# A decoder trunk in float32 parts: 18 of 22 gate and up tiles of each feed-forward block by Strassen's algorithm over halves, and the second product in four sections

## The chip, the cores and the metric

One core of a Trainium2 chip runs the whole program in one launch. The metric is device time in microseconds (us), the median of several runs; the profile is one further execution with the hardware profiler on. TensorE (PE) multiplies, VectorE (DVE), ScalarE (ACT) and GpSimd (POOL) do the elementwise work, and SyncE (SP) issues the large transfers.

## The reference, cut to what matters

Two layers, each a feed-forward block, a mixer and a second feed-forward block: four feed-forward blocks in all. The change touches these; the mixer keeps its arithmetic.

```python
D_MODEL, SEQ, DEPTH, D_FF, FFN_HALF = 1024, 512, 2, 2816, 0.5

def swiglu(h, w_in, w_out):
    gate, up = jnp.split(h @ w_in, 2, axis=-1)
    return (jax.nn.silu(gate) * up) @ w_out

for l in range(DEPTH):
    x = x + FFN_HALF * swiglu(rmsnorm(x, ffn1_norm[l]), ffn1_w_in[l], ffn1_w_out[l])
    x = x + hybrid_mixer(rmsnorm(x, mix_norm[l]), ...)
    x = x + FFN_HALF * swiglu(rmsnorm(x, ffn2_norm[l]), ffn2_w_in[l], ffn2_w_out[l])
```

## The kernel before

Activations lie feature-major: 8 tiles of [128 features, 512 tokens]. Every float32 operand is split into a high and a low part (`wh`, `wl` of a weight, `xh`, `xl` of the stream, `hh`, `hl` of the hidden layer), and a product is three matmuls, high by high, high by low and low by high (`mm3`).

A feed-forward block (`ffn`) has 22 feature tiles of the hidden layer. For each, `proj` makes the gate and then the up tile: 8 row tiles by 3 matmuls of 512 columns each, the weight stationary and the stream moving. The product's bank `pf` is then worked off: `t = pf * r` and `t = pf * t` on DVE, the SiLU on ACT, `t * r` on POOL, and the split into `hh` (ACT) and `hl` (DVE). The second product follows once all 22 are there: 8 output tiles, each a chain of 22 by 3 matmuls of 512 columns in one bank, added to the stream by one DVE instruction.

Weights come through SP, 512 KB at a time, into `raw` (2 slots). `convert` makes `wh` on ACT and `wl = raw - wh` on DVE (3 slots each); so each chunk of [128, 1024] numbers costs one ACT and one DVE instruction beside the 24 matmuls that use it. `convert` runs ahead of the product by these slots.

`Weave` sets the order in which instructions are written out on each engine, with a rough price list: chains of small steps (`weave.spawn`, `yield`) are placed between the matmuls, and `idle` lets work that is not urgent wait for its engine. Each engine then works in that order and waits by semaphores. The mixer uses the same `proj` and also `proj_tm`, whose matmuls have 256 moving columns with the stream stationary.

All instructions go through one recording helper, so that nearly all rows of the profile name its line (L246 here): tiles tell them apart.

Of the kernel before, what the change touches and what calls it, by code (L numbers as in the profile page):

```python
# [40 lines left out]

class Weave:
    """Emission order: chains of small dependent steps between the dense products.

    A chain is a generator that emits a step and yields the time in ns that
    has to pass before its next step beyond what its instructions take. A
    model of the engines, with rough prices of the instructions, tells when
    a chain's last step is through; the dense products, which call tick, fill
    the time in between."""

    COST = {"tensor": (1, 0.417), "vector": (70, 1.04), "scalar": (100, 0.84), "gpsimd": (120, 1.3)}
    HOP = 250.0         # from an engine to what another one does with its result
# [46 lines left out]
    def charge(self, engine, op, outs, ins, func=None):  # L99
# [20 lines left out]
        else:  # L120
# [3 lines left out]
            # columns of scalars, and sums  # L124
# [46 lines left out]
    def both(self, *chains):  # L171
        """One chain out of several."""
# [12 lines left out]
    def after(self, ticket, chain):  # L185
        """The chain, once the last one with this ticket is done."""
# [13 lines left out]
    def then(self, ticket, chain):  # L200
        """The chain, once the last one with this ticket so far is done."""
# [9 lines left out]
    def idle(self, engine, limit=800):  # L211
        """Wait, in a chain, for the engine to run dry, but not for long."""
# [10 lines left out]
class Engine:  # L223
    """An engine whose instructions the model takes down."""
# [26 lines left out]
class Pool:  # L251
    """A tile pool whose tiles the model takes down."""
# [12 lines left out]
    def room(self, tag, bufs=None):  # L265
        """Wait, in a chain, for the next slot of a ring."""
# [18 lines left out]

class Trunk:
    def __init__(self, ctx, tc, depth, w):
        self.tc = tc
        self.nc = self.weave = Weave(tc.nc)
        self.w = w  # L290
# [17 lines left out]
        self.chunks = self.weight_order(depth)  # L308
        self.raws = []
        self.parts = []  # L310
        self.converted = self.used = 0
        self.r = None
        self.evacs = [0, 0]     # of products: called for, emitted
# [8 lines left out]
    def select(self, name, compare, base, cm, step, out=None):  # L322
        """A mask: 1 where base + cm * partition + step * column compares so with 0."""
# [11 lines left out]
    def columns(self, name, ap):  # L335
        """Per-feature vectors, turned so that features lie on partitions."""
# [22 lines left out]
    def more_constants(self, vecs, a_log, dt_bias):  # L359
# [15 lines left out]
        # rows of the identity by quarter: [32 q + blk, a, i] = (i == 8 q + a)  # L375
# [7 lines left out]
        # a_log and dt_bias on every partition  # L383
# [25 lines left out]
    def load_x(self, x, gain):  # L409
        """The stream, feature-major, and with it the first two units of the first product."""  # L410
# [3 lines left out]
        with self.pool("xin", 1) as xin:  # L414
# [9 lines left out]
            for k in range(KD + 4):  # L424
# [11 lines left out]
                # the second unit two tiles behind the first  # L436
# [5 lines left out]
            self.used += 2  # L442
# [47 lines left out]
    def finish_norm(self):  # L490
        """r = (mean of squares + eps) ** -0.5 on every partition; one Newton step."""
# [20 lines left out]
    def weight_order(self, depth):  # L512
        """(matrix, first row tile, row tiles, first column, columns) in the order of use."""
        w = self.w

        def ffn(w_in, w_out):
            for f in range(KF):
                yield w_in, 0, KD, f * P, P
                yield w_in, 0, KD, DFF + f * P, P
            for n in range(KD):  # L520
                for k0, nk in OUT_SPLIT:
                    yield w_out, k0, nk, n * P, P
# [34 lines left out]
    def ahead(self):  # L557
        """Have the oldest chunk that has been fetched split into hi and lo parts."""
        self.weave.spawn(self.weave.after("hi", self.convert()))

    def split_chunk(self, engine):
        """The same at once, the low part by the engine given."""
        nc = self.nc
        raw = self.raws.pop(0)
        self.converted += 1
# [5 lines left out]
        return wh, wl  # L571

    def convert(self):
        nc = self.nc
        if not self.raws:
            return
        # a slot is free once the products with what it held have been emitted
        while self.converted - self.used >= 3:
            yield 300
        self.converted += 1  # L580
        raw = self.raws.pop(0)
        nk, n = raw.shape[1], raw.shape[2]
        if n == 16:
            # few columns: the parts side by side, for two passes over x instead of three
            both = self.wp.tile([P, nk, 2 * n], F32R, tag="wh", bufs=3, name="wb")
            wh, wl = both[:, :, 0:n], both[:, :, n:2 * n]
        else:
            wh = self.wp.tile([P, nk, n], F32R, tag="wh", bufs=3, name="wh")
            wl = self.wp.tile([P, nk, n], F32R, tag="wl", bufs=3, name="wl")
# [3 lines left out]
        def lo():  # L593
            yield from self.weave.idle("vector", LO_WAIT)
            nc.vector.tensor_tensor(wl, raw, wh.bitcast(F32), op=ALU.subtract)
            self.parts.append((wh, wl) if n > 16 else (both, None))
            self.fetch()
# [22 lines left out]
    def bank(self, shape, n=1):  # L620
        """A bank for a product, when n are free."""
# [3 lines left out]
    def evac(self, engine, f):  # L625
        """f, which reads the bank of a product, when the engine has time."""
# [8 lines left out]
    def proj(self, xs=None, units=1):  # L635
        """The next chunks of P columns, feature-major; the last row tile of all comes last."""
        xh, xl = xs or (self.xh, self.xl)
        ws, pss = [], []
        for u in range(units):
            wh, wl = self.next_weights()  # L640
            ps = self.bank([P, SEQ])
            last = KD if units == 1 else KD - 1
            for k in range(last):
                if k == 2:
                    self.ahead()
                self.used += k == KD - 1
                self.weave.until(lambda: len(xl) > k and xl[k] is not None)
                self.mm3(ps, (wh[:, k, :], wl if wl is None else wl[:, k, :]), (xh[k], xl[k]), k == 0, k == KD - 1)
            ws.append((wh, wl))
            pss.append(ps)  # L650
        if units > 1:
            k = KD - 1
            self.weave.until(lambda: len(xl) > k and xl[k] is not None)
            for (wh, wl), ps in zip(ws, pss):
                self.mm3(ps, (wh[:, k, :], wl if wl is None else wl[:, k, :]), (xh[k], xl[k]), False, True)
            self.used += units
        return pss if units > 1 else pss[0]

    def proj_tm(self, ready=lambda: True):
        """256 columns, token-major: two PSUM tiles [P, 2, 256], tokens (2 a + b) P + p."""  # L660
        nc = self.nc
        out = [self.bank([P, 2, 256], 2) for _ in range(2)]
        for k0 in (0, 4):
            wh, wl = self.next_weights()
# [15 lines left out]
            self.used += 1  # L680
# [4 lines left out]
    def ffn(self, hid, finish, first=None):  # L685
        nc = self.nc
        hh, hl = [], []
        first = first or self.proj(units=2)
        self.need_r()
        r = self.r  # L690

        def hidden(f, t):
            h = hid.tile([P, SEQ], F32R, name=f"hh{f}")
            l = hid.tile([P, SEQ], F32R, name=f"hl{f}")
# [815 lines left out]
```

## Time and profile before

| | |
|---|---|
| runs timed | 3, median 2834.55 us (2833.79 to 2834.58) |
| span of the profiled execution | 2834.2 us |
| busy share of the span | PE 99%, weight loads 83%, DVE 56%, ACT 45%, POOL 11% |
| granted TensorE clock | 0.998 of 2.4 GHz over the whole span |
| moved by transfers | 312 MB, mean 110 GB/s |
| stretch of a feed-forward block | about 360 us, four times |
| stretch of a mixer | about 680 us, twice |

The page gives no time for the profiled execution but its span, from its first to its last instruction; that is 0.35 us under the median of the timed runs, so span and time are taken as one number below. Busy shares are means over stages; PE's busy time includes the overlap of matmuls that follow each other, whose ends are modelled. The pace of matmuls is therefore read from the distance of their starts.

### The profile page before, as it was taken

The numbers are of one execution on the slowest core, as the hardware profiler recorded it, in microseconds if no ns is written. First come the engines' busy times: TensorE is split into PE (matmuls) and PEld (weight loads), VectorE is DVE, ScalarE is ACT, GpSimd is POOL, SyncE is SP. The second block draws the span as 40 slices with busy tenths as digits, with TensorE's granted clock in tenths as the row PEclk, the third lists the DMA queues.
The fourth block names the chain that finished last, engine by engine and source line by source line (L and its number), as shares of the span: only waits on it lengthen the run. The fifth ranks groups of instructions, "written<-read, shape, count | busy, mean of one in ns | idle before, by whom it ended". The sixth has DMA issues, their size and how long they took to land.

```text
span 2834.2 us, 38189 instructions
## 1 busy us (share of the span) xinstructions
PE 2803.1 (99%) x14638; PEld 2366.0 (83%) x14638; DVE 1578.3 (56%) x2646; ACT 1267.8 (45%) x2663; POOL 315.4 (11%) x312
## 2 busy tenths in 40 slices
PE   8999999999999999999999999999999999999999
PEld 6888888888888888888888888889988888888887
DVE  5444356987777544443344433678878765544422
ACT  4322236767664543222232222368675745422221
POOL 2110010000100031110011100110001002311100
PEclk9999999999999999999999999999999999999999
DMA  4333333323335743333333333323323349333332
GB/s 128 90 98 102 114 96 88 94 79 88 91 96 178 241 153 93 97 97 97 98 96 97 97 106 107 105 81 84 102 79 99 106 149 302 92 104 97 97 106 80
DMA packets 511223, 312.09 MB, mean 110 GB/s; under 512 B 31050, under 2 KB 481344, under 8 KB 511040
## 3 DMA queue, kind: packets, MB, share of 16 engines
q1 hardware_dynamic: 510704, 309.51, 37.1%
q8 instruction: 116, 1.90, 0.3%
q14 instruction: 67, 0.55, 0.1%
q10 hardware_dynamic: 336, 0.13, 0.0%
HBM read 276.03 MB, written 33.55 MB: 109 GB/s over the span
## 4 chain that ended last, share of the span: by engine, by line
PE 90%; DVE 6%; ACT 3%; issue 1%; DMA 0%; POOL 0%; SPq 0%; DVEq 0%; ACTq 0%; POOLq 0%
PE pf L246 82%; PE sbo_ps L246 1%; ACT u L246 1%; DVE sbs L246 1%; PE pq L246 1%; DVE itmp L246 1%; DVE wl L246 1%; DVE qkv L246 1%; PE z_ps L246 1%; PE pa L246 1%; DVE it L246 1%; PE at_ps L246 1%; PE pp L246 0%; PE py L246 0%; PE qk_ps L246 0%
## 5 line engine op out<-in xcount | busy, mean ns | idle before, releaser
L246 DVE TENSOR_TENSOR wl<-raw,wh 128x1024 fp32r<-128x1024 f32 (+1 forms) x463 | 596.4, 1288 | 484.8 <-ACT wh L246 483.1
L246 PE MATMUL pf<-xh,wh 128*128 128x512 f32 x2176 | 854.4, 393 | 0.2 <-DVE t L246 0.2
L246 PE MATMUL pf<-xh,wl 128*128 128x512 f32 x2176 | 852.4, 392 | 1.6 <-DVE wl L246 1.6
L246 PE MATMUL pf<-xl,wh 128*128 128x512 f32 x2176 | 853.4, 392 | 0.0
L246 ACT ACTIVATE wh<-raw 128x1024 fp32r<-128x1024 f32 (+1 forms) x464 | 481.1, 1038 | 294.2 <-PE pf L246 228.1
L246 PEld LDWEIGHTS pf<-xh,wl 128*128 128x128 f32 x2176 | 409.0, 188 | 88.1 <-DVE wl L246 3.9
L246 PEld LDWEIGHTS pf<-xh,wh 128*128 128x128 f32 x2176 | 409.2, 188 | 83.5 <-issue 1.1
L246 PEld LDWEIGHTS pf<-xl,wh 128*128 128x128 f32 x2176 | 409.2, 188 | 83.2 <-issue 1.4
L246 PE MATMUL pf<-hl,wh 128*128 128x512 f32 x704 | 274.5, 390 | 0.0
L246 PE MATMUL pf<-hh,wh 128*128 128x512 f32 x704 | 273.9, 389 | 0.0
L246 PE MATMUL pf<-hh,wl 128*128 128x512 f32 x704 | 273.9, 389 | 0.0
L246 PE MATMUL pf<-wh,xh 128*128 128x256 f32 x768 | 226.3, 295 | 0.0
L246 PE MATMUL pf<-wl,xh 128*128 128x256 f32 x768 | 218.2, 284 | 0.0
L246 PE MATMUL pf<-wh,xl 128*128 128x256 f32 x768 | 218.0, 284 | 0.0
L246 POOL TENSOR_TENSOR t<-t,r 128x512 f32<-128x512 f32 x88 | 114.1, 1296 | 816.4 <-ACT t L246 816.4
L246 ACT ACTIVATE t<-t 128x512 f32<-128x512 f32 x88 | 55.6, 632 | 330.8 <-DVE t L246 330.8
L246 ACT ACTIVATE hh<-t 128x512 fp32r<-128x512 f32 x88 | 55.6, 632 | 321.9 <-DVE t L246 321.9
L246 PEld LDWEIGHTS pf<-hh,wl 128*128 128x128 f32 x704 | 132.2, 188 | 27.4
L246 PEld LDWEIGHTS pf<-hh,wh 128*128 128x128 f32 x704 | 132.2, 188 | 27.3
L246 PEld LDWEIGHTS pf<-hl,wh 128*128 128x128 f32 x704 | 132.2, 188 | 27.2
L246 PEld LDWEIGHTS pf<-wh,xl 128*128 128x128 f32 x768 | 148.0, 193 | 1.7
L246 PEld LDWEIGHTS pf<-wh,xh 128*128 128x128 f32 x768 | 147.9, 193 | 1.8
(1049 smaller groups left out, 3621.0 us busy)
## 6 DMA issues: line engine op xcount, KB each, us to landing
raw<-in_ffn_w_in_dram SPq DMA_DIRECT2D x176, 512.0 KB, 3.9
raw<-in_w_in_dram SPq DMA_DIRECT2D x144, 512.0 KB, 3.9
raw<-in_ffn_w_out_dram SPq DMA_DIRECT2D x64, 512.0 KB, 4.1
raw<-in_ffn_w_out_dram SPq DMA_DIRECT2D x32, 384.0 KB, 3.4
gsp<-gt SPq DMA_DIRECT2D x32, 256.0 KB, 3.3
of<-osp SPq DMA_DIRECT2D x32, 256.0 KB, 4.3
raw<-in_w_branch_b_dram SPq DMA_DIRECT2D x16, 512.0 KB, 4.2
raw<-in_w_branch_a_dram SPq DMA_DIRECT2D x16, 512.0 KB, 5.2
```

The source lines that it names most:

```text
L246: return f(*args, **kw)
```

## The change

Of the 22 gate and up tile pairs of a block, 4 stay as they were. The other 18 are done two at a time in 9 groups. For a group, the weights are taken as 2 by 2 blocks (gate and up by the two halves of the 1024 inputs, each [4 row tiles, 256 columns]) and the stream as 2 by 2 blocks (halves of the inputs by halves of the 512 tokens). The Winograd form of Strassen's algorithm makes the product from 7 block products in place of 8. Each is 2 feature tiles by 4 row tiles by 3 matmuls of 256 columns: 168 matmuls of 256 columns for a group, in place of 96 of 512.

For this the four weight blocks of a group (`sraw`, 8 slots) get four sums on POOL (`sums`, `last_sum`), and each of the 7 operands is split by `convert` into `wh` and `wl`. The stream is normalized at the start (`xs`, on DVE), its four sums are made on POOL, and the high and low parts of the sums (`halves`) and of the normalized stream (`replace`) are made once a block. Products gather in the banks `pq`, `ps` and `pf`; partial results are copied out by ACT (`m1`, `u2`, `u3`) or added by DVE (`t`, `up1`).

The second product comes in four sections of 4, 6, 6 and 6 hidden tiles, the first before the groups, the others between and after them, each added to the stream by DVE. `PLAN` sets this order. Weights of the second product and of the groups use a fourth pair of slots. In the mixer the one step that reads the beta and decay columns goes through the queue of evacuations.

```diff
-OUT_SPLIT = ((0, 8), (8, 8), (16, 6))
+H = SEQ // 2
+FC = 4
+NQ = (KF - FC) // 2
+SECTIONS = ((0, 4), (4, 6), (10, 6), (16, 6))
+RAWQ = 8
+HOME = {1: 11, 2: 12, 3: 12, 4: 22, 5: 0, 6: 11, 7: 21}
...
+    plan = [("c", u) for u in range(2 * FC)]
+    plan += down(0, (0, 1), 2) + down(0, range(2, KD))
+    plan += [("s", 0, 1), ("s", 0, 5)]
+    for q in range(NQ - 1):
+        plan += [("s", q, 2), ("s", q, 6), ("s", q + 1, 1), ("s", q, 7), ("s", q + 1, 5), ("s", q, 4), ("s", q, 3)]
+        if q in (3, 6):
+            plan += down(q // 3, range(KD))
...
+    def sums(self, q):
...
+        nc.gpsimd.tensor_tensor(t[0], t[21], t[22], op=ALU.add)
...
+        nc.gpsimd.tensor_tensor(t[21], t[11], t[21], op=ALU.subtract)
...
+        while 1 not in f.events:
+            yield 300
+        nc.gpsimd.tensor_tensor(t[11], t[0], t[11], op=ALU.subtract)
...
+    def last_sum(self, q):
...
+        self.nc.gpsimd.tensor_tensor(t[12], t[12], t[11], op=ALU.subtract)
...
+    def halves(self, hid):
...
+            nc.vector.scalar_tensor_tensor(xs[k // 4][:, k % 4, :], self.x[k], self.gain(k), self.r,
+                                           op0=ALU.mult, op1=ALU.mult)
...
+        for i, a, b in ((7, b22, b12), (5, b12, b11), (6, b22, b12), (4, b21, raw[6])):
+            yield 0
+            nc.gpsimd.tensor_tensor(raw[i], a, b, op=ALU.subtract)
...
+    def replace(self):
...
+            nc.scalar.activation(xh, src, AF.Copy)
+            yield 0
+            nc.vector.tensor_tensor(xl, src, xh.bitcast(F32), op=ALU.subtract)
...
+    def of_four(self, ps, i, start):
...
+                for n, (w, x) in enumerate(((wh, xh), (wh, xl), (wl, xh))):
+                    nc.tensor.matmul(ps[:, f, :], w[:, k, cols], x, start=start and f + k + n == 0,
+                                     stop=k == 3 and n == 2, skip_group_check=True)
...
+            if i == 1:
+                s["Q"] = self.sps.tile([P, 2, H], F32, tag="sp", name="pq")
+                self.of_four(s["Q"], 1, True)
+                s["m1"] = small("m1")
+                nc.scalar.copy(s["m1"], s["Q"])
...
+            elif i == 6:
+                self.of_four(s["Q"], 6, False)
+                s["u2"] = small("u2")
+                nc.scalar.copy(s["u2"], s["Q"])
...
+                    nc.scalar.copy(u3, s["Q"])
+                    s["up1"] = small("up1")
+                    nc.vector.tensor_tensor(s["up1"], s["S"], u3, op=ALU.add)
...
+            elif i == 4:
+                self.of_four(s["Q"], 4, False)
+                t = s["g0"]
+                nc.vector.tensor_tensor(t, s["Q"], t, op=ALU.mult)
```

On DVE, in the steady part of the gate and up tiles of the first block: before, the rows of one hidden tile (two chunks of weights, two steps on the bank `pf`, one low part `hl`).

```order
L246 TENSOR_TENSOR wl<-raw,wh 128x1024
L246 TENSOR_TENSOR t<-pf,r 128x512
L246 TENSOR_TENSOR wl<-raw,wh 128x1024
L246 TENSOR_TENSOR t<-pf,t 128x512
L246 TENSOR_TENSOR hl_899<-t,hh_898 128x512
```

In the change, the rows of one whole group at the same place (`sraw` and `s` are weight blocks and their sums, `hp` the hidden layer's parts, `u`, `m` and `up` partial results).

```order
L279 TENSOR_TENSOR t<-pf,m_1010 128x512
L279 TENSOR_TENSOR wl<-sraw,wh 128x1024
L279 TENSOR_TENSOR hp<-t,hp 128x2x256
L279 TENSOR_TENSOR wl<-s_1066,wh 128x1024
L279 TENSOR_TENSOR wl<-sraw,wh 128x1024 x2
L279 TENSOR_TENSOR up_1277<-ps,u_1275 128x512
L279 TENSOR_TENSOR wl<-sraw,wh 128x1024 x2
L279 TENSOR_TENSOR t<-pq,t 128x512
L279 TENSOR_TENSOR hp<-t,hp 128x2x256
L279 TENSOR_TENSOR t<-ps,u_1209 128x512
L279 TENSOR_TENSOR wl<-sraw,wh 128x1024
L279 TENSOR_TENSOR t<-t,up_1277 128x512
```

Two hidden tiles took 10 DVE rows before, 4 of them low parts of weights; a group for two hidden tiles takes 14, 7 of them low parts of weights, and the steps on the banks stand between these in one order.

On POOL, in the first block: before, the last constants, then the gate's `t * r` of 16 hidden tiles, then the sums of squares that follow the block.

```order
L246 MEMSET i_732 128x256
L246 AFFINE_SELECT i_732<-i_732 32x256 x4
L246 TENSOR_TENSOR t<-t,r 128x512 x16
L246 TENSOR_TENSOR ssq<-ssq,sq 128x512 x7
L246 MEMSET zero 128x128
```

In the change, at the same place, the sums of the weight blocks of two groups and a half.

```order
L279 AFFINE_SELECT i_792<-i_792 32x256 x4
L279 TENSOR_TENSOR s_819<-sraw 128x1024
L279 TENSOR_TENSOR sraw<-sraw 128x1024 x2
L279 TENSOR_TENSOR sraw<-s_819,sraw 128x1024
L279 TENSOR_TENSOR s_1066<-sraw 128x1024
L279 TENSOR_TENSOR sraw<-sraw 128x1024 x2
L279 TENSOR_TENSOR sraw<-s_1066,sraw 128x1024
```

Where one instruction on 512 columns stood for a hidden tile, four on 1024 columns stand for a group of two.

On ACT, in the change, between the product 5 of one group and the copy `u3` of the next (`wh` are the high parts of weights, here of a sum and of blocks):

```order
L279 ACTIVATE wh<-s_1066 128x1024
L279 COPY u_1209<-pq 128x512
L279 ACTIVATE wh<-sraw 128x1024
L279 COPY m_1243<-pq 128x512
L279 ACTIVATE wh<-sraw 128x1024
L279 COPY u_1275<-pq 128x512
```

The copies out of the bank `pq`, before which TensorE may not go on in that bank, stand behind high parts of weights that are themselves waiting for sums and slots; before, no copy of this kind stood in a block.

## Rows read from the trace of the kernel before

**Rows 1.** The page: busy time, share of the span and instructions by engine.
```profile
PE 2803.1 (99%) x14638; PEld 2366.0 (83%) x14638; DVE 1578.3 (56%) x2646; ACT 1267.8 (45%) x2663; POOL 315.4 (11%) x312
```

**Rows 2.** Engines by stretch (feed-forward blocks and mixers): us, busy us, clock, DMA share, GB/s.
```profile
35.00:386.00 351.00, 350.99 (x1542) 287.26 (x1543) 144.40 (x158) 104.86 (x132) 43.16 (x43) 1.00 0.35 101
386.00:1066.00 680.00, 671.96 (x4104) 582.74 (x4103) 490.15 (x1004) 417.22 (x1061) 76.82 (x85) 1.00 0.41 121
...
1427.00:1787.00 360.00, 360.00 (x1587) 296.56 (x1586) 148.70 (x156) 105.74 (x133) 37.77 (x32) 1.00 0.35 101
```

**Rows 3.** The chain that ended last: start, us, what, number of matmuls.
```profile
635.99 7.20 PE pf L246 x60
...
1427.79 359.12 PE pf L246 x1584
```

**Rows 4.** Groups by line on TensorE: shape, count, busy us, mean ns, idle before.
```profile
L246 PE MATMUL pf<-xh,wh 128*128 128x512 f32 x2176 | 854.4, 393 | 0.2 <-DVE t L246 0.2
...
L246 PE MATMUL pf<-wh,xh 128*128 128x256 f32 x768 | 226.3, 295 | 0.0
```

**Rows 5.** Groups by line and form on DVE, ACT and POOL, 1428 to 1787 us.
```profile
L246 DVE TENSOR_TENSOR wl<-raw,wh 128x1024 fp32r<-128x1024 f32 x59 | 77.5, 1313 | 93.6 <-ACT wh L246 93.6
L246 DVE TENSOR_TENSOR hl<-t,hh 128x512 fp32r<-128x512 f32 x22 | 15.2, 692 | 14.7 <-ACT hh L246 14.7
L246 DVE TENSOR_TENSOR t<-pf,t 128x512 f32<-128x512 f32 x22 | 15.2, 692 | 37.4 <-PE pf L246 35.3 <-POOL t L246 2.1
...
L246 DVE SCALAR_TENSOR_TENSOR xl<-x,v_nm,xh 128x512 fp32r<-128x512 f32 x8 | 6.0, 752 | 6.3 <-ACT xh L246 6.3
L246 DVE SCALAR_TENSOR_TENSOR x<-pf,x 128x512 f32<-128x512 f32 x8 | 5.5, 691 | 15.2 <-PE pf L246 15.2
...
L246 ACT ACTIVATE wh<-raw 128x1024 fp32r<-128x1024 f32 x59 | 61.8, 1049 | 55.3 <-PE pf L246 54.5 <-DMA raw<-in_ffn_w_in_dram 0.8
L246 ACT ACTIVATE hh<-t 128x512 fp32r<-128x512 f32 x22 | 13.9, 632 | 82.1 <-DVE t L246 82.1
...
L246 POOL TENSOR_TENSOR t<-t,r 128x512 f32<-128x512 f32 x22 | 28.5, 1293 | 205.7 <-ACT t L246 205.7
```

**Rows 6.** Groups by line over the span: a POOL instruction of 1024 columns; an ACT copy from a bank.
```profile
L246 POOL TENSOR_TENSOR wl<-raw,wh 128x1024 fp32r<-128x1024 f32 x1 | 2.4, 2388 | 11.2 <-ACT wh L246 11.2
...
L246 ACT COPY sraw<-pf 128x512 f32<-128x512 f32 x32 | 20.2, 630 | 0.0
```

**Rows 7.** Timeline of DVE and POOL where both work: start us, us, instruction.
```profile
13.32 0.75 DVE L246 SCALAR_TENSOR_TENSOR xl<-xps,v_n,xh 128x512 fp32r<-128x512 f32 x1 [1.41 <-ACT xh L246]
...
13.99 0.68 DVE L246 COPY x<-xps 128x512 f32<-128x512 f32 x1
...
980.79 1.29 POOL L246 TENSOR_TENSOR ga<-ga,yb 128x512 f32<-128x512 f32 x1 [1.32 <-DVE ga L246]
980.80 2.36 DVE L246 TENSOR_TENSOR wl<-raw,wh 128x1024 fp32r<-128x1024 f32 x1 [0.15 <-ACT wh L246]
...
1001.23 1.30 POOL L246 TENSOR_TENSOR yb<-yb,gb 128x512 f32<-128x512 f32 x1 [1.78 <-ACT gb L246]
1001.71 0.69 DVE L246 TENSOR_TENSOR ga<-pf,ga 128x512 f32<-128x512 f32 x1 [0.88 <-PE pf L246]
1002.52 1.23 DVE L246 TENSOR_TENSOR wl<-raw,wh 128x1024 fp32r<-128x1024 f32 x1
1002.60 2.28 POOL L246 TENSOR_TENSOR ga<-ga,yb 128x512 f32<-128x512 f32 x1
```

**Rows 8.** Transfers by issue: queue, count, size, median us from issue to landing.
```profile
raw<-in_ffn_w_in_dram SPq DMA_DIRECT2D x176, 512.0 KB, 3.9
```

More of the change, by code (lines that the diff above doesn't have):

```diff
@@ L679, in proj_tm, with fetch_fours @@
                         self.ahead()
-            self.used += 1
+            used[0] = True
         self.weave.until(ready)
         return out
-    def ffn(self, hid, finish, first=None):
-        nc = self.nc
-        hh, hl = [], []
+    def fetch_fours(self):
+        while True:
+            while self.held and (self.held[0][0] is None or self.held[0][0].free(self.held[0][1])):
+                self.held.pop(0)
+            if not self.blocks or len(self.held) >= self.allowed:
+                return
+            q, b = self.blocks.pop(0)
+            if b == 11:
+                self.fours.append(Four())
+            raw = self.hid.tile([P, 4, 2 * P], F32, tag="sraw", bufs=RAWQ, name="sraw")
+            k0, c0 = (b % 10 - 1) * 4 * P, (b // 10 - 1) * DFF + (FC + 2 * q) * P
+            self.nc.sync.dma_start(
+                raw, self.w_in[k0:k0 + 4 * P, c0:c0 + 2 * P].rearrange("(k p) n -> p k n", p=P))
+            four = self.fours[q]
+            four.tiles[b] = raw
+            self.held.append((four, b))
+            if b == 22:
+                self.weave.spawn(self.weave.after("sums", self.sums(q)))
+            if b == 12:
+                self.weave.spawn(self.weave.after("last sum", self.last_sum(q)))
@@ L688, in ffn @@
+    def ffn(self, hid, w_in, w_out, finish, first=None):
+        nc = self.nc
+        pairs = {}
+        self.hid, self.w_in, self.w_down = hid, w_in, w_out
+        self.nhid = 0
+        self.fours = []
+        self.blocks = [(q, b) for q in range(NQ) for b in (11, 21, 22, 12)]
         first = first or self.proj(units=2)
@@ new lines, in ffn, with pair, hidden @@
+        self.sums_x = [(i, hid.tile([P, 4, 2 * P], F32, tag="sraw", bufs=RAWQ, name="sx")) for i in (7, 6, 4)]
+        self.held = [(Four(), -i) for i, _ in self.sums_x]
+        self.allowed = 3
+        self.weave.spawn(self.weave.after("halves", self.halves(hid)))
+        done = set()
+        state = {}
+        def pair(p):
+            if p not in pairs:
+                pairs[p] = hid.tile([P, 2, 2, SEQ], F32R, tag="hp", bufs=4, name="hp")
+            return pairs[p]
+        def hidden(hi, lo, t, key):
+            nc.scalar.activation(hi, t, AF.Copy)
+            yield 0
+            nc.vector.tensor_tensor(lo, t, hi.bitcast(F32), op=ALU.subtract)
+            done.add(key)
@@ new lines, in tile, with small, plain @@
+        def tile():
+            return self.stat.tile([P, SEQ], F32, tag="out", bufs=3, name="t")
+        def small(name):
+            return self.stat.tile([P, 2, H], F32, tag="sq", bufs=SQ, name=name)
+        def plain(u):
+            f = u // 2
+            ps = first[u] if u < 2 else self.proj()
+            if u % 2 == 0:
+                t = state["t"] = tile()
+                nc.vector.tensor_mul(t, ps, r)
+                nc.scalar.activation(t, t, AF.Silu)
+                nc.gpsimd.tensor_mul(t, t, r)
+            else:
+                t = state["t"]
+                nc.vector.tensor_mul(t, ps, t)
+                h = pair(f // 2)
+                self.weave.spawn(self.weave.after("x", hidden(h[:, 0, f % 2, :], h[:, 1, f % 2, :], t, f)))
+                self.allowed = min(RAWQ, self.allowed + 2)
+                self.fetch_fours()
@@ new lines, in second, with ready, down @@
+        def second(q, t, up):
+            nc.vector.tensor_tensor(t, t, up, op=ALU.mult)
+            yield 0
+            h = pair(FC // 2 + q)
+            yield from hidden(h[:, 0, :, H:], h[:, 1, :, H:], t, (q, 1))
+        def ready(f):
+            return f in done if f < FC else {((f - FC) // 2, 0), ((f - FC) // 2, 1)} <= done
+        def down(sec, n, k0, k1):
+            f0, nf = SECTIONS[sec]
+            if k0 == 0:
+                state["d", n] = self.next_weights(), self.bank([P, SEQ])
+                if (sec, n) != (len(SECTIONS) - 1, KD - 1):
+                    self.ahead()
+            (wh, wl, used), ps = state["d", n]
+            for k in range(k0, k1):
+                f = f0 + k
+                self.weave.until(lambda: ready(f))
+                h = pairs[f // 2]
+                self.mm3(ps, (wh[:, k, :], wl[:, k, :]), (h[:, 0, f % 2, :], h[:, 1, f % 2, :]), k == 0, k == nf - 1)
+            if k1 == nf:
+                used[0] = True
+                nc.vector.scalar_tensor_tensor(self.x[n], ps, 0.5, self.x[n], op0=ALU.mult, op1=ALU.add)
+                if sec == len(SECTIONS) - 1:
+                    finish(n)
@@ L726, in small_rsqrt @@
+        later = None
+        for item in PLAN:
+            if item[0] == "d" and later is None:
+                later = True
+                self.weave.until(lambda: self.weave.done("halves"))
+                self.ahead()
+                self.weave.spawn(self.replace())
+            if item == ("s", 0, 1):
+                self.weave.until(lambda: self.weave.done("constants"))
+            {"c": plain, "s": four, "d": down}[item[0]](*item[1:])
+        self.hid = None
     def small_rsqrt(self, y, v, t):
```

251 lines of the change are left out of this document (179 added, 72 removed).

## The prediction, made before the changed kernel was run

> **What bounds the kernel now.** I read the page first, then the stretches, then the chain that ended last, then the groups of each engine. TensorE is busy 99% of the span [rows 1]. The stretches say where it isn't: in the mixers (8 us in the one shown); in the feed-forward blocks it is busy 360.00 of 360.00 us, with DVE at 149, ACT at 106 and POOL at 38 us [rows 2]. The chain agrees: a whole block is one piece, 1584 matmuls in 359.12 us with nothing else in it [rows 3]. So a block is bound by the number of matmuls times their distance, 359.12 / 1584 = 0.2267 us, and whatever takes matmuls away there shortens the program one for one, as long as the other engines keep up. The mean duration of one, 393 ns [rows 4], is its passage through the array and not its distance. Profiled span (2834.2 us) and median of the runs (2834.55) are one number here; 0.2%, or 5.7 us, is about what a measurement of this kernel can tell from no change.
>
> **What the change removes.** For two hidden tiles, 4 x 24 = 96 matmuls of 512 columns: 96 x 0.2267 = 21.76 us. **What it adds in their place:** 7 x 24 = 168 matmuls of 256 columns. Their distance is on record in the mixer, where 60 of this shape (also with a new stationary operand for each) take 7.20 us: 0.1200 us [rows 3, 4]. So 168 x 0.12 = 20.16 us. A group saves 1.60 us; 9 groups in 4 blocks save 57.7 us. Note how little of the eighth that Strassen removes is left: 168 half matmuls at half of 0.2267 would be 19.04 us, and 1.1 us of 2.7 go to the 6.6 ns that each half matmul costs above a half. The distance at which nothing would be won is 21.76 / 168 = 0.1295 us.
>
> A page's figure speaks against this. The Trainium skill ("TensorE: Matmul & The Clock Gate", section "Back-to-back issue gap") gives sustained distances of about 81 ns at 128 columns and 131 ns at 512; an estimate on the line between them is 98 ns at 256. By it a group would cost 168 x 98 = 16.4 us against 96 x 131 = 12.6, and the change would lose 3.8 us a group, 138 us in all. The trace has 226.7 and 120.0 ns for these operands, so it doesn't bear the figure out.
>
> The second product has the same 528 matmuls in four sections, nothing removed. Its price is 24 more additions to the stream in a block, 0.69 us each [rows 5]; they lie beside sections of 12 to 18 matmuls a tile (2.7 to 4.1 us), in which DVE has one more instruction or two, and there are three banks. I put them at nothing; without that cover they would be 16.6 us a block. Transfers: the same bytes, in rows twice as long, at a third of the engines' time [rows 2], 3.9 us from issue to landing [rows 8]; a block of weights is asked for as soon as one of the eight slots comes free. Nothing. The moved step of the mixer: one instruction on 32 partitions, nothing.
>
> **What the other engines must do in 20.16 us.** This is the part that decides. A group on ACT: 7 high parts at 1.05, three copies at 0.63, four steps at 0.63 [rows 5, 6]: 11.8 us. DVE: 7 low parts at 1.23 when undisturbed [rows 7] and 7 steps at 0.69: 13.4 us. POOL: 4 sums at 2.39 [rows 6]: 9.6 us, where it had 2 x 1.29. Each fits alone. But POOL and DVE are not independent. At 1002.52 a low part (two inputs from SBUF) runs on DVE, and POOL's instruction, issued 0.08 us later, takes 2.28 us in place of 1.29; at 980.79 POOL is first by 0.01 us and the low part takes 2.36 in place of 1.23 [rows 7]. One waits for the other to the end: the pair takes 2.36 where the two durations add up to 2.52. An instruction with one input in a bank is not touched (0.69 us at 1001.71, under a POOL instruction) [rows 7].
>
> Of DVE's 13.4 us a group, 7 x 1.23 + 3 x 0.69 = 10.7 have two inputs in SBUF. With POOL's 9.6 that makes 20.2 us of a resource that only one can hold, for 20.16 us of matmuls. Bounds for the time by which a group is late: from below 0, if POOL's sums fall into DVE's 6.8 idle us and its 2.8 us on banks. From above, everything in a row is 13.4 + 9.6 = 23.0 us, 2.8 too long. Taking off what neighbours overlap (0.08 us between two on DVE, as at 13.99, for 13 pairs; 0.16 for 4 meetings with POOL) [rows 7] it is 21.4, 1.2 too long. I take **0.6 us a group**, half of the 1.2: four slots of weights let a low part be some three products (8.6 us) early, so single meetings are hidden, but with the port full a queue that is late once stays late, and the order rows show the bank steps locked between the low parts in one order. Only the sections of the second product, where POOL has little to do, give time back. 36 x 0.6 = 21.6 us.
>
> **The start of a block.** Between the norm and the first group there are 144 matmuls of plain tiles and 96 of section 0: 240 x 0.2267 = 54.4 us. With two inputs in SBUF DVE has 8 normalizations at 0.75, 12 low parts of the stream and the hidden layer at 0.69, 3 of sums and some 7 of weights at 1.23, and 8 of half size (as `hl`, 0.69): 32.1 us [rows 5, 7]. POOL has 4 x 1.29 and, with four sums of the stream, the first group's first three and half of the second's, 9 x 2.39: 26.7 us. Together 58.8: up to 4.4 us too much, if none can slide, and nothing, if the second group's sums do. I take 1 us a block: 4 us.
>
> **Sum.** 2834.2 - 57.7 + 21.6 + 4 = **2802 us**. My own range for this case is 2790 to 2815 (0.25 to 0.95 us a group).
>
> **The rivals.**
> *All hidden.* POOL's sums are needed late (a sum is written out some products ahead of its use), so POOL could work only where DVE doesn't. For it: DVE's sum is 13.4 of 20.16. Against it: the port's 20.2 of 20.16. It gives 2776.5, up to 2788 with a little lost. Chance 0.2.
> *Slower: the two engines in a row.* If a late DVE makes every sum of POOL fall on a low part and nothing overlaps, a group takes 23.0 us, 36 x 2.8 = 101 us are lost and the time is 2834 - 58 + 101 + 4 = 2881. From 1.6 us a group on (less the start, 1.5) the change loses. Against it: a POOL instruction can start under any of four bank steps, and DVE idles while it waits for ACT. The Trainium skill ("GPSIMD Engine Reference", section "1. Specifications") names contention with DVE instructions that have two SBUF inputs; the meetings of [rows 7] agree, and give its size. Chance 0.09.
> *Late copies on ACT.* Product 7 may only go on in its bank when ACT has copied `u2`, one product (2.9 us) after it is there, and product 4 when `u3` is copied. Both copies stand behind high parts that wait for POOL's sums and for slots, and behind a hidden part that waits for DVE. Each lateness of DVE then comes back through ACT: 0.5 us a group more, 18 us: 2820. For it: the order rows; against it: ACT is idle 8 us a group. Chance 0.13.
> *Half matmuls dearer than in the mixer.* Here the weights are stationary and two of three matmuls in a row load the same ones. If the distance were 0.135 us, a group would take 22.7 us: 0.92 us dearer than before, 33 us, and with the 26 us lost 2893. The rows of the mixer speak against any price above 0.1295. Chance 0.03.
> *No change.* Lost time of some 1.5 us a group would eat just what is won. Chance 0.05.
>
> **How the numbers follow.** Forecast 0.50, all hidden 0.20, late copies 0.13, no change 0.05, slower 0.12. Faster: 0.83; same: 0.05; slower: 0.12. The range for 8 in 10 takes in the first three: 2777 (the matmuls alone) to 2828 (late copies, and half of what the start can cost beyond my 1 us: 4 x 1.7).
>
> **What would show it.** Per block 1512 matmuls of 256 columns 0.12 us apart, and pieces of them in the chain broken by short idle times of TensorE whose releasers are `wl` on DVE or `u2`, `u3` on ACT. The mean of the low parts of `sraw` above 1.3 us, or POOL's sums above 2.39: the meetings. In the first groups of a run little idle time, more in the third and fourth, if lateness adds up. A distance other than 0.12 would make the first term wrong; idle time behind transfers (`sraw`) would be a cause that I put at nothing; a mixer that is longer or shorter by more than 3 us likewise.

## The result: 28 us faster, and the profile after

The changed kernel takes 2806.58 us (median of 4 runs, 2805.78 to 2808.63) against 2834.57 us for the kernel before on the same chip: a ratio of 0.9903, 95% interval 0.9889 to 0.9917. Its profiled span is 2803.9 us, 30.3 less than before and 1.9 more than forecast.

The page's busy row answers to [rows 1]:

```profile
PE 2750.8 (98%) x17230; PEld 2441.1 (87%) x17230; DVE 1998.8 (71%) x2994; ACT 1466.4 (52%) x2955; POOL 681.7 (24%) x400
```

The stretches, as in [rows 2], but from the start of one block's or mixer's norm to the next. Columns: stretch, its length, busy time of PE, weight loads, DVE, ACT and POOL with instructions, granted clock, share of the DMA engines, GB/s.

```profile
27.00:381.00 354.00, 344.95 (x2214) 311.88 (x2215) 253.86 (x251) 156.57 (x208) 135.00 (x65) 1.00 0.33 98
381.00:1059.70 678.70, 670.14 (x4104) 580.96 (x4102) 490.33 (x1005) 416.90 (x1062) 76.55 (x85) 1.00 0.41 122
1059.70:1413.10 353.40, 348.94 (x2242) 318.31 (x2243) 253.70 (x243) 156.39 (x206) 130.16 (x51) 1.00 0.33 100
1413.10:1765.90 352.80, 347.63 (x2235) 315.74 (x2234) 253.18 (x243) 155.72 (x206) 130.04 (x54) 1.00 0.34 102
1765.90:2444.60 678.70, 670.12 (x4104) 581.03 (x4102) 490.30 (x1005) 417.29 (x1062) 76.56 (x85) 1.00 0.41 122
2444.60:2803.90 359.30, 350.83 (x2256) 318.64 (x2256) 242.25 (x232) 147.55 (x194) 119.38 (x44) 0.99 0.32 96
```

In the kernel before, the same stretches last 356.9, 679.8, 361.9, 360.0, 680.3 and 367.2 us. So the first block wins 3 us and the other three 7 to 8.5; none wins the 14.4 (9 x 1.60) that the matmuls save. TensorE is idle for 4.5 to 9.1 us in a block, where the two blocks of [rows 2] showed at most 0.01 (in the fourth block 4.8 of 8.5 us are the end of the program, which cost 4.7 before too).

Where that idle time is not: in the steady groups. Of the chain that ended last (start, duration, what), two pieces one group apart; then the windows of a whole group and of 230 us from 90 us behind the norm on:

```profile
1158.55 8.64 PE pq L279 x72
...
1178.71 8.64 PE pq L279 x72
```

```profile
1158.55:1178.71 20.16, 20.16 (x171) 20.16 (x170) 17.74 (x15) 10.84 (x14) 11.30 (x4) 1.00 0.33 104
1149.70:1379.70 230.00, 230.00 (x1649) 218.15 (x1649) 161.22 (x149) 100.81 (x129) 79.84 (x29) 1.00 0.30 90
```

72 matmuls of 256 columns take 8.64 us, 0.1200 each, the distance of [rows 3]; the pieces start 20.16 us apart, which is 168 x 0.12 to the hundredth. In none of the four blocks does any matmul from 90 to 320 us behind the norm start more than 0.03 us later than this pace (0.2267 us for 512 columns) lets it. DVE was to be busy 13.4 us a group when undisturbed; it is busy 17.8. So the meetings with POOL are there, and they cost TensorE nothing. A group of DVE's instructions (busy time, mean ns of one, idle before and its releaser) shows whom they hit:

```profile
L279 DVE TENSOR_TENSOR wl<-sraw,wh 128x1024 fp32r<-128x1024 f32 x216 | 377.3, 1757 | 64.3 <-ACT wh L279 64.3
```

The low parts of the groups' weights take 1757 ns in the mean, where one takes 1.23 us undisturbed [rows 7].

Where the idle time is: TensorE's waits (what, us in total, times, longest).

```profile
PE pf L279 <- DVE wl L279: 12.9, 10, 2.6
...
PE vp L279 <- DMA vt<-in_dn_out_norm_dram: 3.7, 1, 3.7
...
PE pq L279 <- ACT u L279: 3.0, 4, 0.9
...
PE adt_ps L279 <- DMA adt_row<-in_dn_dt_bias_dram: 1.2, 1, 1.2
```

But for 1.3 us of the first row, in the mixers, all lie within 85 us of a block's norm. The third block, 22 to 65 us after its norm; first POOL (five of its nine instructions), then DVE, ACT and TensorE (start, duration, instruction, idle before and its releaser):

```profile
1435.65 5.06 POOL L279 TENSOR_TENSOR sx<-xs 128x1024 f32<-128x1024 f32 x1 [3.88 <-DVE xs L279]
...
1447.63 2.85 POOL L279 TENSOR_TENSOR sraw<-sraw 128x1024 f32<-128x1024 f32 x1
1450.43 2.85 POOL L279 TENSOR_TENSOR sx<-xs 128x1024 f32<-128x1024 f32 x1
1453.26 1.29 POOL L279 TENSOR_TENSOR t<-t,r 128x512 f32<-128x512 f32 x1
1454.51 3.32 POOL L279 TENSOR_TENSOR sx<-xs,sx 128x1024 f32<-128x1024 f32 x1
1478.12 2.41 POOL L279 TENSOR_TENSOR sraw<-s,sraw 128x1024 f32<-128x1024 f32 x1 [20.28 <-DVE wl L279]
```

```profile
1445.33 0.69 DVE L279 TENSOR_TENSOR t<-pf,t 128x512 f32<-128x512 f32 x1 [1.18 <-POOL t L279]
1446.72 1.50 DVE L279 TENSOR_TENSOR hp<-t,hp 128x512 fp32r<-128x512 f32 x1 [0.70 <-ACT hp L279]
1448.14 2.88 DVE L279 TENSOR_TENSOR wl<-raw,wh 128x512 fp32r<-128x512 f32 x1
1450.95 0.68 DVE L279 TENSOR_TENSOR t<-pf,r 128x512 f32<-128x512 f32 x1
1453.28 2.35 DVE L279 TENSOR_TENSOR tl<-sx,th 128x1024 fp32r<-128x1024 f32 x1 [1.65 <-ACT th L279]
1455.55 2.83 DVE L279 TENSOR_TENSOR wl<-raw,wh 128x512 fp32r<-128x512 f32 x1
```

```profile
1451.66 0.63 ACT L279 ACTIVATE t<-t 128x512 f32<-128x512 f32 x1 [4.45 <-DVE t L279]
1452.20 1.05 ACT L279 ACTIVATE th<-sx 128x1024 fp32r<-128x1024 f32 x1
```

```profile
1455.27 0.61 PE L279 MATMUL pf<-hp,wh 128*128 128x512 f32 x2
1458.44 0.50 PE L279 MATMUL pf<-hp,wl 128*128 128x512 f32 x1 [2.55 <-DVE wl L279]
```

POOL works 22 us without a pause, then rests for 20. `wl` of a 512-column chunk, 0.69 us alone (as `hl` in [rows 5]), takes 2.88 and 2.83, and between the two DVE stands 1.65 us before a `tl`. That one waits for `th`, which stands on ACT behind a SiLU (`t`), which waits for DVE's `t<-pf,r`, which had to wait for the first stretched `wl`: a late engine is late once more through its own queue. The second `wl` of section 0 ends at 1458.4; TensorE has waited 2.55 us for it. By the distances of the matmuls' starts, blocks 2 and 3 lose 4.2 us each to this and the waits for `hp` just behind it, and 0.8 to 1.9 in the first group. The fourth block loses as much in section 0, but after its wait of 2.5 us TensorE works on at the lower clock and the waits for `hp` are missing (last section).

### The profile page after: what moved, and what is told of

The parts are those of the page before. It is cut to its first block, busy times and chain, and to the rows that moved or that the text cites. A ratio compares the mean times of both kernels' runs of the same rounds, so it can differ in the third digit from the quotient of the medians.

```text
span 2803.9 us, 44397 instructions
## 1 busy us (share of the span) xinstructions
PE 2750.8 (98%) x17230; PEld 2441.1 (87%) x17230; DVE 1998.8 (71%) x2994; ACT 1466.4 (52%) x2955; POOL 681.7 (24%) x400
## 4 chain that ended last, share of the span: by engine, by line
PE 79%; DVE 10%; issue 4%; ACT 3%; POOL 2%; DMA 1%; SPq 0%; DVEq 0%; POOLq 0%; ACTq 0%
PE pf L279 51%; PE pq L279 15%; PE ps L279 7%; DVE wl L279 3%; ACT u L279 1%; DVE itmp L279 1%; DVE sbs L279 1%; PE sbo_ps L279 1%; DVE qkv L279 1%; POOL t L279 1%; DVE it L279 1%; PE z_ps L279 1%; PE pa L279 1%; PE at_ps L279 0%; PE pp L279 0%
## 5 line engine op out<-in xcount | busy, mean ns | idle before, releaser
L279 DVE TENSOR_TENSOR wl<-raw,wh 128x1024 fp32r<-128x1024 f32 (+2 forms) x351 | 430.8, 1228 | 138.4 <-ACT wh L279 135.7
L279 ACT ACTIVATE wh<-raw 128x1024 fp32r<-128x1024 f32 (+2 forms) x352 | 336.9, 959 | 300.6 <-PE pf L279 149.9
L279 PE MATMUL pf<-xh,wl 128*128 128x512 f32 (+1 forms) x1312 | 486.1, 371 | 5.3 <-DVE wl L279 5.3
L279 PE MATMUL pf<-xh,wh 128*128 128x512 f32 (+1 forms) x1312 | 487.0, 371 | 0.2 <-DVE t L279 0.2
L279 PE MATMUL pf<-xl,wh 128*128 128x512 f32 (+1 forms) x1312 | 486.7, 371 | 0.0
L279 PE MATMUL pf<-hp,wh 128*128 128x512 f32 x1408 | 439.3, 392 | 2.1 <-DVE hp L279 1.1
L279 DVE TENSOR_TENSOR wl<-sraw,wh 128x1024 fp32r<-128x1024 f32 x216 | 377.3, 1757 | 64.3 <-ACT wh L279 64.3
L279 PEld LDWEIGHTS pf<-hp,wh 128*128 128x128 f32 x1408 | 264.6, 189 | 58.3 <-DVE hp L279 2.2
L279 PE MATMUL pf<-hp,wl 128*128 128x512 f32 x704 | 276.0, 392 | 7.6 <-DVE wl L279 7.6
L279 PE MATMUL pq<-th,wh 128*128 128x256 f32 x864 | 244.9, 283 | 3.0 <-ACT u L279 3.0
```

The source lines that it names most:

```text
L279: return f(*args, **kw)
```

## The experiments

Theory: in the steady groups the meetings of POOL and DVE are hidden; at the start of a block they are not, and that is where the time is given back. Rivals: they cost time in the groups after all; DVE simply has too much work at the start; or the sections themselves wait. All edits are to the changed kernel (2806.6) unless said otherwise.

| run | median us | ratio to before, 95% interval |
|---|---|---|
| e2, no later sums | 2803.04 | 0.9891 (0.9874 to 0.9907) |
| e3, one extra sum | 2859.63 | 1.0088 (1.0073 to 1.0103) |
| e3, two extra sums | 2896.92 | 1.0222 (1.0208 to 1.0236) |
| e7, sections alone | 2835.69 | 1.0003 (0.9993 to 1.0012) |
| e1, first sums late | 2808.80 | 0.9908 (0.9893 to 0.9922) |
| e5, stream's sums on DVE | 2801.53 | 0.9886 (0.9871 to 0.9901) |
| e4, constants early | 2806.87 | 0.9903 (0.9889 to 0.9918) |
| e8, e5 with e4 | 2794.32 | 0.9856 (0.9840 to 0.9873) |
| e9, e8 with early `xs` | 2800.93 | 0.9881 (0.9866 to 0.9896) |
| e10, e8 with e1 | 2787.18 | 0.9832 (0.9819 to 0.9846) |

The intervals of e1, e2, e4 and e5 overlap that of the changed kernel (0.9889 to 0.9917), so what these edits do is read from the lengths of the blocks and the waits in their profiles.

**The steady groups (e2, e3).** First without POOL's sums in 32 of the 36 groups:

```diff
-        nc.gpsimd.tensor_tensor(t[0], t[21], t[22], op=ALU.add)
+        if q:
+            t[0] = t[22]
...
+        else:
+            nc.gpsimd.tensor_tensor(t[0], t[21], t[22], op=ALU.add)
...
```

> Edit: the four sums of weights on POOL are left out in all groups but the first of a block (32 of 36); the products take blocks of the weights as they are. This leaves out part of the computation. The order of all other instructions is unchanged. Theory (in the steady groups the meetings of POOL and DVE are hidden behind the slots, and cost TensorE nothing): 2803 to 2807, at most 3 us less. The prediction's step (0.6 us a group are lost to these meetings): 32 x 0.6 = 19 us less, 2787.

2803.0: 3.5 us less. The third block now has 41 us of POOL's work and 221 of DVE's, and is 1.8 us shorter:

```profile
1412.20:1763.20 351.00, 348.00 (x2235) 316.39 (x2234) 220.84 (x243) 156.60 (x206) 41.05 (x22) 1.00 0.34 102
```

The theory holds, and 19 us are not there to be won. Not even the 3.5 us lie in the steady groups: what is gone are the waits in the blocks' first groups, 3.0 us for `u` and 0.5 for `wl` of the groups, since the second group's sums fall there. The waits of 2.5 us in sections 0 are as before. Then the other way, the first sum of a group made twice, and three times:

```diff
+        for _ in range(1 if q else 0):
+            self.tc.nc.gpsimd.tensor_tensor(t[0], t[21], t[22], op=ALU.add)
```

> Edit: in the same 32 groups the first sum on POOL is made twice (the second time with the same result), all else and the order unchanged. POOL then has five sums of 2.4 us a group. The prediction's sum for the port (DVE's 10.7 us with two inputs in SBUF and POOL's sums, in 20.16 us, nothing overlapping): 10.7 + 12.0 = 22.7, so 2.5 us a group late, 32 x 2.5 = 80 us more, 2886. Theory (DVE has some 2 us a group left and can take the fifth meeting of 1.2 us): up to 10 us more, 2806 to 2817.

2859.6: 53 us more, 1.66 us a group. Both expectations missed: the cover was far thinner than the theory had it. TensorE now waits for ACT's copies:

```profile
PE pq L279 <- ACT u L279: 35.0, 22, 3.1
PE pf L279 <- DVE wl L279: 12.9, 10, 2.6
```

The second row is as in the changed kernel (the block starts); the first, 35 us in place of 3, is new: 1.0 us a group. Behind such waits TensorE works at the lower clock more often: the mean granted clock of the profiled run is 0.992, in the changed kernel 0.999, which over 2856 us makes some 20 us (an estimate). The waits and the clock together make up nearly all of the 53 us. So of the extra 2.4 us between 0.75 (by the time) and 1.4 us (by the waits alone) found room. `u2` is copied by ACT behind other work that waits for DVE: the rival "late copies on ACT" is what comes first once the port is full.

> Edit: as the run with one extra sum of POOL in each of 32 groups, but with two extra ones. One extra sum of 2.4 us made a group 1.6 us longer, so the changed kernel had about 0.8 us of SBUF time left in a group. Theory (POOL's sums and DVE's instructions with two inputs in SBUF take turns without overlap, and the free time is used up by the first): the second extra sum costs its whole 2.4 us, or 2.2 less the overlap of neighbours: 70 to 77 us more, 2930 to 2937. Rival (DVE can still work on its bank steps under POOL's sums, or waits for other things anyway): about as much as the first, 40 to 60 us more, 2900 to 2920.

2896.9: the second extra sum costs 37.3 us, 1.17 us a group. That is less than either expectation, about half of its duration. The waits for `u` grow to 40.2 us, waits for low parts of the groups' weights come in, and the mean clock is 0.989:

```profile
PE ps L279 <- DVE wl L279: 18.8, 11, 2.9
```

So the plain sum of the two engines' durations does not say what an overfull port costs; part of the second sum lies under work that doesn't need the port or under waits that are there already, and the runs don't say which.

**The sections alone (e7)**, on the kernel before:

```diff
-OUT_SPLIT = ((0, 8), (8, 8), (16, 6))
+SECTIONS = ((0, 4), (4, 6), (10, 6), (16, 6))
+AFTER = {5: 0, 11: 1, 17: 2}
...
+            if f in AFTER:
+                section(AFTER[f])
+        section(3)
```

> Edit: the kernel before, with only the second product changed: four sections of 4, 6, 6 and 6 hidden tiles after the hidden tiles 5, 11, 17 and 21, each added to the stream; all gate and up tiles plain. The prediction's step (24 more additions and 8 more pairs of conversions a block cost nothing): 2833 to 2837. Rival (each section starts or ends with a wait, as the waits of 2.5 us in section 0 of the changed kernel may be the section's own): 2 to 5 us a block more, 2842 to 2854.

2835.7, a ratio of 1.0003. DVE's work in the third block grows by 15 us (163.98 against 148.70 in [rows 2]), and TensorE stays busy throughout:

```profile
1428.10:1787.30 359.20, 359.17 (x1582) 296.02 (x1583) 163.98 (x187) 107.16 (x140) 38.52 (x32) 1.00 0.35 101
```

So the waits in section 0 are not the section's own. TensorE's only new wait among the blocks is one of 1.15 us for a sum of squares on POOL, at the end of the second.

**The start of a block (e1, e5).** First the first group's sums, moved into POOL's idle 20 us:

```diff
+        while q == 0 and not self.weave.done("halves"):
+            yield 300
         nc.gpsimd.tensor_tensor(t[0], t[21], t[22], op=ALU.add)
```

> Edit: in each block the first group's sums of weights on POOL wait until the four sums of the stream are through, so that POOL works on into the 19 us (1106 to 1125 in the third block's neighbour, the second block) in which it was idle, and fewer of its instructions meet DVE's at the start of the block. Theory (the start of a block loses its 6 to 7 us because POOL and DVE take turns at SBUF there, and low parts of section 0's weights come late): the stall of 2.5 us on `wl` falls by half or more and the time falls by 8 to 18 us, to 2789 to 2799. Rival (DVE has simply too much work there, whatever POOL does): 2804 to 2809, unchanged. Third way: the first group's operands are late instead, and TensorE waits before the first `pq` products: 2806 or more.

2808.8, a miss. The waits in section 0 did fall, from 4.2 to 2.9 and 2.8 us in the second and third block, but the stream's four sums still met DVE's instructions. The third block won 1.6 us, the second and fourth 0.1 and 0.5 (the second's first group gave back 1.0 of the 1.2 that its section 0 had won), and the first lost 1.9, nearly all to waits for transfers of constants. Then those sums themselves, on DVE:

```diff
-            nc.gpsimd.tensor_tensor(raw[i], a, b, op=ALU.subtract)
+            nc.vector.tensor_tensor(raw[i], a, b, op=ALU.subtract)
```

> Edit: the four sums of the stream at the start of a block are made on DVE in place of POOL, where they take 2.4 us each and their meetings stretch DVE's low parts to 2.8 us. In the changed kernel the blocks 2 to 4 lose 4.2 us each while section 0 is multiplied (waits for `wl` and `hp`) and 1.1 to 1.9 us in the first group. Theory (turn-taking of POOL and DVE at SBUF, and instructions that stand behind it in their queues): the waits in section 0 shrink below 1 us, 10 to 15 us less, 2792 to 2797. Rival (DVE has too much work there): DVE gets 4 x 1.23 = 4.9 us more just there, and each block gets longer by 2 to 5 us, 2814 to 2827.

2801.5, 5 us less. The blocks 2 to 4 win 2.5, 3.6 and 2.5 us with more work on DVE, so it isn't DVE's amount of work; the turn-taking holds. The expected 10 to 15 were too much: waits for `wl` that cost 0.9 and 1.4 us stay in the plain tiles of blocks 2 to 4. The first block, on the other hand, became 3.1 us longer: TensorE waited 7.1 us at 91 us for the transfer of `adt_row`. The edit doesn't touch that transfer, but the transfer isn't what is slow. ACT issues it at 97.4 us, after it has stood 7.83 us for the constant `gt`, which POOL makes, and in this order POOL had two sums of the second group ahead of `gt`, the last at 94.27 us (in the changed kernel ACT stood 4.43 us for `gt`):

```profile
94.27 2.34 POOL L279 TENSOR_TENSOR sraw<-sraw 128x1024 f32<-128x1024 f32 x1 [1.16 <-DVE wl L279]
...
96.83 0.29 POOL L279 TENSOR_SCALAR_AFFINE_SELECT gt<-gt 128x128 f32<-128x128 f32 x1
```

```profile
97.15 0.30 ACT L279 CAST m_gt<-gt 128x128 fp32r<-128x128 f32 x1 [7.83 <-POOL gt L279]
...
97.43 0.26 ACTq L279 DMA_DIRECT2D adt_row<-in_dn_dt_bias_dram  x1
```

So TensorE waits for POOL's sums once more, by way of ACT's queue. With the constants earlier this should go.

**The first block (e4, e8).**

```diff
-    ], dn_a_log, dn_dt_bias)), 20000)
+    ], dn_a_log, dn_dt_bias)), 4000)
```

> Edit: the constants of the mixer are prepared from 4 us on in place of 20 us after the program's start, as the modelled clock has it. In the changed kernel TensorE waits 3.7 us at 69.8 us for a transfer of one of them (`vt`) and 1.3 us at 92.9 for another (`adt_row`), and the granted clock is 0.83 in the stretch 70 to 80 us that follows. Theory (these stalls are the reason that the first block wins 3 us where the others win 7 to 8): 3 to 7 us less, 2800 to 2803.5, all of it in the first block. Rival (the waits only show time lost elsewhere, to low parts that are late in the first block): 2805 to 2808.

2806.9, no gain. The first block did win 2.7 us (354.0 to 351.2), but the first mixer lost 2.1 and the second block 0.6. In the mixer two windows of 20 us have a granted clock of 0.91, where the changed kernel has none and the kernel before had one: such dips move with small changes in the order, and what they cost fits the 2.1 us (last section).

> Edits: the stream's sums on DVE and the constants 16 us earlier, together. The earlier constants took 2.7 us off the first block when alone, and gave it back in the first mixer (680.8 in place of 678.7 us). If both edits act independently and the theory of the turn-taking holds: 2 to 3 us less than with the sums on DVE alone, 2789 to 2795. Rival (what the constants save in the first block comes back in the mixer every time): the same as with the sums on DVE alone, within 1 us.

2794.3: 7.2 us below e5, for the first block is 348.6 in place of 357.1 us. The gain is larger than the single edits had shown, because `adt_row` no longer comes late: ACT now issues it at 84.1 us, and TensorE doesn't wait for it.

**Early `xs` (e9).**

```diff
-            yield from self.weave.idle("vector", 1500)
+            yield 0
             nc.vector.scalar_tensor_tensor(xs[k // 4][:, k % 4, :], ...
```

> Edits: as the run with both, and the eight normalizations of the stream are written out in a row in place of each waiting for an idle DVE. The stream's sums can then start some 6 us earlier. Theory (the start loses time to what comes late in section 0): 1 to 4 us less than with both. Rival (six us of DVE in a row push back the steps of the plain tiles, whose banks TensorE then waits for): 2 to 8 us more than with both.

2800.9, the rival: 6.6 us more than e8. In the second block, three `xs` of 0.75 us take 6.35, and the low part behind them in the queue is late: TensorE waits 2.85 us for it, to 1082.9. The third and fourth block have the same wait, of 2.9 and 2.8 us, followed there by the lower clock (mean over the third block 0.990), and the third is 5.1 us longer than in e8.

```profile
1072.88 6.35 DVE L279 SCALAR_TENSOR_TENSOR xs<-x,v_n,r 128x512 f32<-128x512 f32 x3
...
1081.67 1.22 DVE L279 TENSOR_TENSOR wl<-raw,wh 128x1024 fp32r<-128x1024 f32 x1
```

**All three (e10):** the edits of e5, e4 and e1.

> Edits: the stream's sums on DVE and the constants earlier, as in the run with both (2794.3), and with them the first group's sums on POOL put behind the stream's, as in the first experiment. In the run with both TensorE still waits 0.9 and 1.4 us a block for `wl`, at 26 and 38 us into the block, and a POOL sum lies over the DVE instruction just ahead (5.9 us for four of 0.75; 2.8 for a low part of 1.2). Theory of the turn-taking: these two waits get shorter, 3 to 8 us less than with both, 2786 to 2791. Rival (what is moved meets other DVE work later, as in the first experiment, where half of the stall remained and nothing was won): 2792 to 2797.

2787.2 us, 47 us below the kernel before and 19 below the changed one: the best version found. The blocks are 345.6, 349.8, 348.0 and 356.0 us long; TensorE's waits for `wl` fall from 12.9 to 3.1 us:

```profile
27.50:373.10 345.60, 343.03 (x2214) 310.83 (x2215) 253.10 (x255) 157.15 (x208) 124.11 (x61) 1.00 0.34 100
...
1403.60:1751.60 348.00, 346.68 (x2235) 315.78 (x2234) 254.44 (x247) 155.42 (x206) 117.41 (x50) 1.00 0.34 103
...
2431.60:2787.60 356.00, 349.11 (x2256) 317.69 (x2256) 242.88 (x236) 147.81 (x194) 106.30 (x40) 1.00 0.33 98
```

```profile
PE pf L279 <- DVE wl L279: 3.1, 6, 1.1
```

What won nothing alone (e1) brings 7 us here: 3.0 in the first block, some 1.7 of them (an estimate: 0.5% of 349 us) because a stretch at the lower clock in e8, where the mean of that block is 0.995, has no counterpart in e10, and 1.0 to 1.6 in each of the others. In e8 the first group's two sums lay over DVE instructions ahead of late low parts, four `xs` and a `tl` of the third block (e8, then e10's same `tl`):

```profile
1426.49 5.91 DVE L279 SCALAR_TENSOR_TENSOR xs<-x,v_n,r 128x512 f32<-128x512 f32 x4
...
1443.30 2.82 DVE L279 TENSOR_TENSOR tl<-sx,th 128x1024 fp32r<-128x1024 f32 x1
```

```profile
1435.65 1.21 DVE L279 TENSOR_TENSOR tl<-sx,th 128x1024 fp32r<-128x1024 f32 x1
```

## Why the time was right, and which steps were not

**The matmuls: right.** 0.2267 and 0.1200 us apart, 1.60 us a group. The rivals with dearer half matmuls or no change are out. The page's figure that spoke against the change (the Trainium skill, "TensorE: Matmul & The Clock Gate", section "Back-to-back issue gap"), by which a group would have lost 3.8 us, is not borne out by these operands.

**"I take 0.6 us a group": wrong.** It measured nothing: groups start 20.16 us apart, and what leaving POOL's sums out wins (3.5 us) lies in the first groups. The mechanism before it was right (pairs do take turns, low parts rise to 1757 ns), and its sum of 20.2 us of port time in 20.16 was close: an extra sum shows 0.75 to 1.4 us of room, so 18.8 to 19.4 is used. What failed is the step from a nearly full port to lateness. DVE grows to 17.8 us, less than 20.16, no queue falls behind for good, and the slots of weights ahead of TensorE can cover the single meetings (no run changed their number, so that the slots are what covers them is argued, not shown). The forecast took half of 1.2 us, a sum that still laid POOL's sums end to end with DVE's bank steps, though the row had shown that these are not touched.

**"I take 1 us a block": mis-sized.** Against the 14.4 us, the blocks 2 to 4 gave back 6.0, 7.2 and 6.5 us. The own bound for the start, up to 4.4 us, was the better value: 4.2 went in section 0 of these blocks to what just these meetings made late, and most of the rest in the first group. The estimate compared sums over 54 us. But POOL's work stands in 22 of them, ahead of `t` and `tl` that TensorE's next weights wait behind, and POOL is idle in the 20 that follow.

**The first block: not foreseen.** It gave back 11.5 us: 5 to waits for transfers of constants, 3.7 to two late low parts at 40 and 47 us, 0.6 in the first group, and 1.7 to a lower clock (below). In the kernel before, TensorE's only wait behind the norm of that block is one of 0.2 us for DVE's `t`, which the changed kernel has too. Transfers were put at nothing by looking at the weights; those of the constants, which nothing waited for there, were not looked at. Nor are these transfers slow: ACT issues them late, because it stands for POOL. In the changed kernel the one that TensorE waits for until 73.9 us (`vt`) is issued behind a `th` that waited 3.5 us for one of POOL's sums of the stream:

```profile
69.18 1.06 ACT L279 ACTIVATE th<-sx 128x1024 fp32r<-128x1024 f32 x1 [3.52 <-POOL sx L279]
...
70.87 0.47 ACTq L279 DMA_DIRECT2D vt<-in_dn_out_norm_dram  x1
```

**Put at nothing, and nothing:** the sections (e7). The mixers are 1.1 and 1.6 us shorter, under the 3 us that were named as a sign; each had one dip of the clock in the kernel before and has none now (last section).

So 31.2 us were given back in the blocks, where 25.6 had been put into the sum, and mixers and head returned 3.9. The forecast of 2802 hit by luck: the two errors, 21.6 too many in the groups and some 27 too few at the starts, nearly cancel, and the 3.9, which was not in the sum, takes most of the rest. The forecast's picture of where the time goes was the wrong one: it would have sent an engineer to the steady groups, where there is nothing to win, and not to the starts, where e10 wins 19.

Two small sums of the prediction are off: with its own figures everything in a row less the overlaps is 21.3 us, not 21.4, and the upper end of its range is 2827, not 2828. No step hangs on either.

## What to carry to other kernels

When two engines share a resource, a sum of durations over a stage says whether it can be hidden, not whether it is: look at the places where the work is bunched and what stands behind it in each queue. Moving a bunch to the engine that does it in half the time (1.2 against 2.4 us) can help even when that engine is the busier one. When a block's cover is shortened, go through everything that was placed under it, constants' transfers too. A wait for a transfer can be a wait for the engine that issues it: look at what stands ahead of the issue in that engine's queue.

## What the runs showed of the hardware that was not expected

A wait of TensorE can cost more than itself. In the run with the stream's sums on DVE it waited 7.1 us for `adt_row`, from 91 us on. The granted clock (third number from the end) in the windows around:

```profile
91.00:98.40 7.40, 0.54 (x3) 0.12 (x1) 3.79 (x3) 0.97 (x2) 6.02 (x8) 0.70 0.00 0
98.40:102.00 3.60, 3.37 (x15) 3.30 (x16) 1.74 (x4) 1.77 (x3) 3.30 (x7) 0.50 0.02 5
102.00:106.00 4.00, 4.00 (x27) 4.00 (x27) 0.07 (x1) 1.42 (x2) 2.29 (x1) 0.72 0.42 131
```

TensorE worked on at 1.2 GHz for 3.6 us (0.50), and was back at 2.4 GHz by 106 us: 3.6 x 0.5 + 4 x 0.28 = 2.9 us beside the wait. In the changed kernel the wait of 3.7 us from 70.2 us on is followed by clocks of 0.65 and 0.92:

```profile
70.00:74.00 4.00, 0.29 (x2) 0.11 (x1) 4.00 (x8) 3.38 (x7) 0.00 (x0) 1.00 0.52 162
74.00:78.00 4.00, 4.00 (x13) 3.12 (x14) 3.04 (x6) 0.09 (x1) 0.00 (x0) 0.65 0.76 229
78.00:82.00 4.00, 4.00 (x18) 3.03 (x16) 2.58 (x5) 2.19 (x4) 0.00 (x0) 0.92 0.24 68
```

That is 4 x 0.35 + 4 x 0.08 = 1.7 us more.

The length of a wait alone doesn't decide it. Of the waits of 2.5 us in the changed kernel's sections 0, those of the second and third block (2.49 and 2.55 us) leave the clock at 1.00; that of the fourth (2.54 us, to 2491.8) doesn't:

```profile
2491.80:2495.80 4.00, 3.98 (x10) 2.95 (x11) 4.00 (x6) 2.77 (x6) 0.00 (x0) 0.57 0.64 188
```

That fall cost nothing of its own: the slower matmuls take the place of the waits for `hp` that the other two blocks have behind it, and section 0 loses the same time in all three.

The mixers show the price most clearly, since hardly anything in them is changed. Over the profiles of all the kernels here, a mixer takes 678.7 to 679.3 us where the granted clock doesn't fall, 679.5 to 680.3 where it falls once, and 680.7 to 681.1 where it falls twice. A difference of 1 or 2 us between two kernels whose edits lie elsewhere can be this.
